# A decoder layer with a convolution branch and an attention branch: the order of the work around its norm and its output stage is changed

## The chip, the cores and the metric

The kernel runs on one core of one Trainium2 chip. The metric is the device time of one execution in microseconds (us). Times given as a median come from several executions without the profiler; everything that is read from a profile comes from one further execution, whose own time is given beside its span.

The core has a matrix engine (TensorE, PE in the profile), three elementwise engines (VectorE, DVE; ScalarE, ACT; GpSimd, POOL), a sequencer that issues most transfers (SyncE, SP), and DMA queues. Each engine works through its own list of instructions in order. An instruction that waits holds up all that stand behind it on its engine, and none on another engine unless they wait for its result.

## The reference, cut to what matters

Sequence length and model width are 1024, the batch is 1, all in float32.

```python
mod = c @ w_ada + b_ada
shift, scale, gate = split(mod, 3)
h = rmsnorm(x, norm_g) * (1 + scale) + shift
proj = h @ w_in
(glu_a, glu_b, z_conv, q, k, v, z_att, g_conv, g_att) = split(proj)

u = glu_a * sigmoid(glu_b)
u = causal_depthwise_conv(u, conv_w) + conv_b          # 31 taps for each channel
u = silu(layernorm(u, conv_ln_g, conv_ln_b))
y_conv = (u * silu(z_conv)) @ w_conv_out

q, k = rope(q, positions), rope(k, positions)
att = dilated_window_attention(q, k, v)                # 3 groups of 8 heads, width 64
y_att = (att * silu(z_att)) @ w_att_out

merged = sigmoid(g_conv) * y_conv + sigmoid(g_att) * y_att
out = rmsnorm(x + gate * (merged @ w_o), final_g)
```

## The kernel before, in words

**Products.** Every float32 operand of a projection is split into a high and a low part (`whi`/`wlo` of a weight, `hh`/`hl` of h, `uh`/`ul` of the conv branch), and a product is three matmuls: high by high, high by low, low by high (`mm3`, L72 to L75, and L605). A matmul is 128x128 by 128x512. Twelve of them, four blocks of the inner dimension by three products, make a **group**.

**Stages.** First h is built and the first projection units are computed together with it (to about 95 us). Then comes the middle stage (L420 to L1063, to about 610 us): all that is left of the conv branch, the gates and the values, the depthwise conv, the layernorm over channels and the product with `w_conv_out`. Attention and the last product follow; the change does not touch them.

**The middle stage** is a schedule written as code. `groups` is the list of PE groups in order, one for each step. `todo[step]` holds other work for a step, entered with `at(step, rank, fn)`; ranks run from EARLY over COPY, EVICT, HIGH, POOLED, POST_ to LOAD. `behind` holds generators (above all the conv of a channel tile on DVE, 31 taps each), which after each step are run on for a credit of one group; each piece yields its estimated price (`TAP` 1.33, `POST` 0.76), and `spend` takes from the same credit. So work put before a generator moves all its later pieces. The loop at the end runs step by step and writes every instruction into its engine's list in that order. The list is then fixed: an engine does not pass over an instruction that waits.

**Weights.** `Raw` loads a 128x1024 weight on SP into one of three `wraw` buffers. `Form` makes the split of one half of it: `whi` on ACT three steps before its use (L455), `wlo` on POOL two steps before (L458). Two `Form`s share one pair of tiles, and three pairs go round; a pair is free again when PE has read both halves.

**Around the start of the middle stage.** `first` holds six PSUM banks of the units computed so far, and `p_row` a seventh bank with the row of the shift. `first_units` (from L996) copies that row out on ACT (`gs`, L998), takes the sigmoids of four banks on ACT (L1002, L1005) and multiplies on DVE (`glu_half`, L670), which frees the banks. `t_first` loads combinations of h (`t_loads`, L500 to L504), adds them on DVE (`t_raws`, L508 to L511) and splits them: `t_high` on ACT (L515), `t_low` on DVE (L519). The first PE groups here (`plain`) need a bank that these free.

**The norm over channels.** `norm_mean` sums the eight conv results over channels on PE (`pm`, L775), `norm_squares` subtracts the mean on DVE, squares on ACT and adds up (`tot`, L785 to L793), `col_sums` brings the sums into columns (L128), `rstd_cols` makes 1/sqrt with a square root on ACT (L112) and six small operations on DVE (`lcols`, L113 to L117, L134), and eight transposes on PE spread them into `lrow` (L808). Then `norm_apply` makes for each of eight channel tiles: times `lrow` on DVE (L824), silu in two halves on ACT (L826), times the gate `sz` in two halves on DVE (L834), the high part `uh` on ACT (L837), the low part `ul` on POOL (L841).

**The output stage.** `first_outputs` runs eight steps of 12 matmuls; step k takes channel tile k into four banks (two output tiles d by two halves), so that PE can begin before all eight tiles are there. It needs four banks that the last `values` turn has just filled and that ACT must copy out (`gs`, L614). The six outputs left follow, four groups each. `Gated` multiplies a result by its gate `sgc` on DVE and stores it to `cscr`; it also loads a row block of `w_ada` into a `wraw` buffer and has DVE make the column of `gate` from it (`modulation`, L169) with `cb`, the conditioning vector in all partitions, which stands in slot t7. `tables` computes the sines for the rotation from `posi`.

## Time and profile before

| What | Value |
| --- | --- |
| Time of three runs, us | 1223.71, 1225.28, 1226.23 (median 1225.28) |
| The profiled execution: its time, its span, us | 1226.17, 1224.4 |
| Mean granted TensorE clock of it | 0.993 |
| PE busy, us and share of the span | 1197.1, 98% |
| DVE, ACT, POOL busy, us | 901.6, 587.2, 425.1 |

The profiled execution took 1.8 us more than its span, for what lies before its first and behind its last instruction. It stands 0.89 us above the median. In a row of the timeline the first number is the start in us from the beginning of the span, the second the duration in us, then come engine, line and operation; in brackets stands for how long the engine had been idle before, and which engine and tile ended that. A row with "x2" is two instructions, and its time covers both.

### The profile page before, as it was taken

How to read it: one execution, taken by the hardware profiler on the slowest of the kernel's cores; microseconds unless marked ns; L12 is line 12 of the kernel's file. 1: busy time of each engine (PE TensorE's matmuls, PEld its weight loads, DVE VectorE, ACT ScalarE, POOL GpSimd, SP SyncE). 2: the span in 40 equal slices, each digit the busy share in tenths (PEclk: the TensorE clock that was granted, in tenths of full speed). 3: DMA queues.
4: the chain of work that ended last, by engine and by line, in shares of the span. 5: the costliest groups of instructions: out<-in, count | busy, mean ns of one | idle time of the engine just before them, and what ended most of it. 6: DMA issues, size and time to landing. Idle time of an engine off the chain costs nothing.

```text
span 1224.4 us, 17342 instructions
## 1 busy us (share of the span) xinstructions
PE 1197.1 (98%) x6042; PEld 1000.4 (82%) x6042; DVE 901.6 (74%) x1488; ACT 587.2 (48%) x1209; POOL 425.1 (35%) x316
## 2 busy tenths in 40 slices
PE   9999999999999999898999999999999999999997
PEld 7886888888888887676888888888888888888886
DVE  7879999999999998565236657877877752549544
ACT  5655244544445345721025656656666564445111
POOL 0005868788787775632141011111111111200000
PEclk9999999999999999998999999999999999999999
DMA  9584323322423238536645455665675574668231
GB/s 358 194 321 138 121 97 110 105 82 89 130 68 133 84 137 304 194 126 218 223 114 154 122 147 137 184 167 145 166 190 145 136 194 132 215 225 291 86 103 69
DMA packets 100141, 194.49 MB, mean 159 GB/s; under 512 B 29587, under 2 KB 43219, under 8 KB 100054
## 3 DMA queue, kind: packets, MB, share of 16 engines
q1 hardware_dynamic: 83376, 186.77, 49.3%
q10 hardware_dynamic: 16678, 6.61, 1.9%
q8 instruction: 48, 0.79, 0.3%
q14 instruction: 39, 0.32, 0.1%
HBM read 122.25 MB, written 39.62 MB: 132 GB/s over the span
## 4 chain that ended last, share of the span: by engine, by line
PE 85%; DVE 6%; DMA 3%; ACT 2%; issue 2%; POOL 1%; SPq 0%; ACTq 0%; DVEq 0%; POOLq 0%
PE d L75 20%; PE d L73 20%; PE d L74 20%; PE d L605 4%; PE o L1345 4%; PE d L274 3%; PE s L1308 3%; PE t L1324 3%; PE d L1637 2%; PE d L1636 2%; PE d L1638 2%; DMA wraw<-in_w_co 1%; DVE tot L790 1%; ACT d L826 1%; DVE vt L824 0%
## 5 line engine op out<-in xcount | busy, mean ns | idle before, releaser
L547 DVE SCALAR_TENSOR_TENSOR acc<-u,cw,acc 128x1024 f32<-128x1024 f32 x232 | 298.8, 1288 | 6.6
L73 PE MATMUL d<-hh,whi 128*128 128x512 f32 x752 | 295.1, 392 | 2.4 <-ACT gs L998 1.3
L75 PE MATMUL d<-hh,wlo 128*128 128x512 f32 x752 | 293.6, 390 | 0.2 <-POOL wlo L58 0.2
L74 PE MATMUL d<-hl,whi 128*128 128x512 f32 x752 | 293.4, 390 | 0.0
L458 POOL TENSOR_TENSOR wlo<-wraw,whi 128x512 fp32r<-128x512 f32 x130 | 173.8, 1345 | 235.4 <-ACT whi L455 235.2
L58 POOL TENSOR_TENSOR wlo<-wraw,whi 128x512 fp32r<-128x512 f32 (+1 forms) x56 | 81.7, 1478 | 378.9 <-ACT whi L57 378.9
L75 PEld LDWEIGHTS d<-hh,wlo 128*128 128x128 f32 x752 | 141.1, 188 | 31.1 <-POOL wlo L58 0.6
L73 PEld LDWEIGHTS d<-hh,whi 128*128 128x128 f32 x752 | 141.4, 188 | 29.6 <-ACT gs L998 1.8
L74 PEld LDWEIGHTS d<-hl,whi 128*128 128x128 f32 x752 | 141.3, 188 | 26.0
L455 ACT ACTIVATE whi<-wraw 128x512 fp32r<-128x512 f32 x130 | 79.2, 624 | 120.0 <-DMA wraw<-in_w_co 58.4
L1317 ACT ACTIVATE sb<-sb,stats 128x128 f32<-128x128 f32 (+1 forms) x192 | 84.8, 443 | 31.5 <-DVE stats L1313 31.2
L1313 DVE CUSTOM_DVE_ANT_0 sb<-s,mask 128x128 f32<-128x128 f32 (+1 forms) x192 | 59.7, 349 | 52.6 <-PE s L1308 50.9
L1324 PE MATMUL t<-ident,sb 128*128 128x128 f32 x280 | 73.7, 276 | 0.0
L1345 PE MATMUL o<-ph,vt 128*64 128x128 f32 (+1 forms) x432 | 65.9, 253 | 0.0
L1139 ACT ACTIVATE ph<-t 128x384 fp32r<-128x384 f32 (+2 forms) x96 | 45.7, 476 | 38.9 <-PE t L1324 27.7
L1142 DVE TENSOR_TENSOR pl<-t,ph 128x384 fp32r<-128x384 f32 (+2 forms) x96 | 52.0, 542 | 11.0 <-ACT ph L1139 10.4
L73 PE MATMUL d<-uh,whi 128*128 128x512 f32 x128 | 52.0, 406 | 7.0 <-ACT whi L455 6.1
L1308 PE MATMUL s<-k,ql 128*128 128x128 f32 (+1 forms) x192 | 55.0, 292 | 0.0
L605 PE MATMUL d<-wlo,hh 128*128 128x512 f32 x128 | 50.7, 396 | 3.9 <-POOL wlo L458 3.9
L75 PE MATMUL d<-uh,wlo 128*128 128x512 f32 x128 | 51.8, 404 | 1.3 <-POOL wlo L458 1.1
L1345 PE MATMUL o<-pl,vt 128*64 128x128 f32 (+1 forms) x216 | 52.8, 261 | 0.0
L74 PE MATMUL d<-ul,whi 128*128 128x512 f32 x128 | 51.6, 403 | 0.0
(295 smaller groups left out, 2616.5 us busy)
## 6 DMA issues: line engine op xcount, KB each, us to landing
wraw<-in_w_t SPq DMA_DIRECT2D x67, 512.0 KB, 4.2
k<-kqp SPq DMA_DIRECT2D x96, 128.0 KB, 2.3
q<-kqp SPq DMA_DIRECT2D x96, 128.0 KB, 2.4
wraw<-in_w_v SPq DMA_DIRECT2D x19, 512.0 KB, 4.0
wa<-in_w_ada SPq DMA_DIRECT2D x16, 512.0 KB, 5.9
ql<-kqp SPq DMA_DIRECT2D x48, 128.0 KB, 2.4
wg<-wscr SPq DMA_DIRECT2D x48, 128.0 KB, 3.0
hscr<-x SPq DMA_DIRECT2D x8, 512.0 KB, 4.5
```

The source lines that it names most:

```text
L58: (lo_eng or nc.vector).tensor_sub(lo, raw, hi.bitcast(F32))
L73: nc.tensor.matmul(ps, lh, rh, start=start, stop=False, skip_group_check=again)
L74: nc.tensor.matmul(ps, lh, rl, start=False, stop=False, skip_group_check=again)
L75: nc.tensor.matmul(ps, ll, rh, start=False, stop=stop, skip_group_check=again)
L455: nc.scalar.activation(self.hi, src(), AF.Copy)
L458: nc.gpsimd.tensor_sub(self.lo, src(), self.hi.bitcast(F32))
L547: nc.vector.scalar_tensor_tensor(acc, u[:, k:k + S], cw[:, ct, k:k + 1], acc, op0=mult, op1=add)
L605: nc.tensor.matmul(ps[i], l[:, k, c], r, start=k == 0 and n == 0, stop=k == KT - 1 and n == 2)
L1308: products.append((w, lambda c=c, w=w, l=x[:, ts_], r=k[:, ks], i=i: nc.tensor.matmul(ps[:, c:c + w], l, r, start=i == 0, stop=i == 1)))
L1317: nc.scalar.activation(sb[:, c:c + w], sb[:, c:c + w], AF.Exp, bias=stats[:, t, h, 1:2], scale=-1.0, accum_out=stats[:, t, h, 0:1])
L1324: yield from ((lambda c=c: nc.tensor.transpose(ps[:, c:c + P], sb[:, c:c + P], ident)) for c in range(0, o, P))
L1345: nc.tensor.matmul(out_, l, r, **kw))
```

## The change

1. **Start of the middle stage.** `first_units` enters the four sigmoids first on ACT, then the `t_high` splits, then the copy of `p_row`. `t_low` is taken out of `t_first` and entered one step later, each with `spend(TAP)`. A one-element sigmoid is put in front of `t_loads`. `plain` takes its two banks in the other order. Slots of the pool are created in another order, and `t_loads` uses other slots.
2. **Norm.** A one-element square root is entered after the last square, and a one-element silu after the square root of the columns, each of which makes ACT load that function's table there.
3. **norm_apply.** The product with `lrow` of tile ct+1 is entered before the gate products of tile ct, its silu before the copy `uh` of tile ct; the `ul` subtractions are entered one step later.
4. **Weight forms.** The four halves of the first two `w_conv_out` tiles are paired by inner half (kh), no longer by output tile, and made at step + kh.
5. **Output stage.** The gate's column sums move out of `Gated` into `gate_sum`, which loads its part of `w_ada` into slot t7 and stands at step + 7 + 3d. The `sgc` loads are entered two steps later. `cb`, `posi`, `n_` and `m_` change their slots, and `cb` is loaded 12 steps earlier.

The core of the diff:

```diff
-    for x in ("n2", "n4", "h3", "l3"):
-        slot(x, "t")
-    piece("t", "gs", 4)
-    for x in ("n3", "s1", "sd0", "sd1", *(f"t{n}" for n in range(16))):
+    slot("h3", "t"), slot("l3", "t"), piece("t", "gs", 4)
+    for x in ("n3", "s1", "sd0", "sd1", "n2", "n4", *(f"t{n}" for n in range(16))):
         slot(x, "t")
...
-                if i == 0:
-                    ps[half] = bank()
+                if i == half == 0:
+                    ps[1], ps[0] = bank(), bank()
...
+        nc.scalar.activation(one_b[:, 0:1], ones[:, 0:1], AF.Sqrt)
         nc.vector.tensor_add(tot2, tot2, last)
...
         lcols = rstd_cols(pc, "l")
+        nc.scalar.activation(one_b[:, 0:1], ones[:, 0:1], AF.Silu)
...
         for ct in range(KT):
+            if ct + 1 < KT:
+                scaled_mul(ct + 1)
+                yield TAP
             for half in range(2):
                 s = wide(half)
                 nc.vector.tensor_mul(vt[ct][:, s], sg[half], sz_t[ct][:, s])
             yield 2 * POST
+            if ct + 1 < KT:
+                silu(ct + 1)
...
             nc.scalar.activation(hi, vt[ct], AF.Copy)
-            if ct + 1 < KT:
-                scaled_(ct + 1)
-                yield TAP
-            nc.gpsimd.tensor_sub(lo, vt[ct], hi.bitcast(F32))
             ch[ct], cl[ct] = hi, lo
+            at(now[0] + 1, POOLED, lambda ct=ct: nc.gpsimd.tensor_sub(cl[ct], vt[ct], ch[ct].bitcast(F32)))
...
-            at(step - 2, LOAD, self.load)
+            at(step, LOAD, self.load)
...
-            self.wa = load_raw(a["w_ada"][2 * KT + self.d])
...
+    def gate_sum(step, d):
+        box = []
+
+        def load():
+            box.append(slot("t7", "wada"))
+            nc.sync.dma_start(box[0], a["w_ada"][2 * KT + d])
+
+        def post():
+            modulation(2 * KT + d, gate_c[:, d:d + 1], box[0], box[0], cb_of[0])
+            spend(TAP)
+        at(step - 2, LOAD, load)
+        at(step, POST_, post)
...
-        raws = [Raw(step - 7 + d, a["w_co"][d]) for d in range(2)]
-        forms = {(d, kh): Form(step - 3 + 2 * kh + d, raws[d].half(kh)) for kh in range(2) for d in range(2)}
-        out = [Gated(step + 6 + d, d) for d in range(2)]
+        raws = [Raw(step - 7 + 2 * d, a["w_co"][d]) for d in range(2)]
+        forms = {(d, kh): Form(step + kh, raws[d].half(kh)) for kh in range(2) for d in range(2)}
+        out = [Gated(step + 5, d) for d in range(2)]
+        for d in range(KT):
+            gate_sum(step + 7 + 3 * d, d)
...
     def t_first():
+        nc.scalar.activation(one_b[:, 0:1], ones[:, 0:1], AF.Sigmoid)
         t_loads(0)
         t_raws(0)
-        for i in (1, 3, 2, 4):
-            t_high(i, 0)
-            t_low(i, 0)
...
     def first_units():
-        b_row = piece("gs", "gs", 4)[0:2]
-        nc.scalar.activation(b_row, p_row, AF.Copy)
-        nc.scalar.dma_start(bscr, b_row)
         sb = slot("n4", "sigb")
...
+        for i in (1, 3, 2, 4):
+            t_high(i, 0)
+        b_row = piece("gs", "gs", 4)[0:2]
+        nc.scalar.activation(b_row, p_row, AF.Copy)
+        nc.scalar.dma_start(bscr, b_row)
...
-    at(len(groups), LOAD, cb_load)
+    at(len(groups) - 12, LOAD, cb_load)
...
-    at(-1, HIGH, t_first)
+    at(-4, EARLY, t_first)
+    at(1, POST_, t_lows)
```

The lists of three engines show it. First ACT at the start of the middle stage, before: `t1h` to `t4h` are the splits, `gs` is the copy of `p_row`, `sigb` are the sigmoids.

```order
L455 ACTIVATE whi<-wraw 128x512 x2
L515 ACTIVATE t1h_855<-traw 128x1024
L515 ACTIVATE t3h_859<-traw 128x1024
L515 ACTIVATE t2h_863<-traw 128x1024
L515 ACTIVATE t4h_867<-traw 128x1024
L998 ACTIVATE gs<-d 2x512
L999 DMA bscr<-gs 2x512
L1002 ACT_TABLE_LOAD
L1002 ACTIVATE sigb<-d 128x512 x2
L1005 ACTIVATE sigb<-d 128x512 x2
```

The same place on ACT after the change.

```order
L453 ACTIVATE whi<-wraw 128x512 x2
L1016 ACT_TABLE_LOAD
L1016 ACTIVATE sigb<-d 128x512 x2
L1019 ACTIVATE sigb<-d 128x512 x2
L513 ACTIVATE t1h_862<-traw 128x1024
L513 ACTIVATE t3h_864<-traw 128x1024
L513 ACTIVATE t2h_866<-traw 128x1024
L513 ACTIVATE t4h_868<-traw 128x1024
L1023 ACTIVATE gs<-d 2x512
L1024 DMA bscr<-gs 2x512
```

The sigmoids and their table load moved ahead of the four splits, and the copy of `p_row` now stands behind both. The table load is still there.

Second, ACT from the square root of the columns (`ltmp`) to the fourth silu, before: `d<-vt` is a silu of two halves, `uh` a high part, `gs` are the copies that free the four banks of the last `values` turn.

```order
L112 ACTIVATE ltmp<-lcols 128x8
L455 ACTIVATE whi<-wraw 128x512 x2
L826 ACT_TABLE_LOAD
L826 ACTIVATE d<-vt_3697,cvec 128x512 x2
L837 ACTIVATE uh_3993<-vt_3697 128x1024
L826 ACTIVATE d<-vt_3699,cvec 128x512 x2
L455 ACTIVATE whi<-wraw 128x512 x2
L837 ACTIVATE uh_4022<-vt_3699 128x1024
L826 ACTIVATE d<-vt_3701,cvec 128x512 x2
L455 ACTIVATE whi<-wraw 128x512
L837 ACTIVATE uh_4048<-vt_3701 128x1024
L826 ACTIVATE d<-vt_3703,cvec 128x512 x2
```

And after the change.

```order
L112 ACTIVATE ltmp<-lcols 128x8
L803 ACT_TABLE_LOAD
L803 ACTIVATE one_b<-ones 128x1
L453 ACTIVATE whi<-wraw 128x512 x2
L832 ACTIVATE d<-vt_3694,cvec 128x512 x2
L832 ACTIVATE d<-vt_3696,cvec 128x512 x2
L848 ACTIVATE uh_4027<-vt_3694 128x1024
L453 ACTIVATE whi<-wraw 128x512 x2
L832 ACTIVATE d<-vt_3698,cvec 128x512 x2
L848 ACTIVATE uh_4056<-vt_3696 128x1024
L612 ACTIVATE gs<-d 128x512 x4
L832 ACTIVATE d<-vt_3700,cvec 128x512 x2
```

The table load moved ahead of the two weight splits, the silu of the next tile ahead of `uh`, and the four `gs` copies, which stood behind the fifth silu (two tiles further on), now stand behind the second `uh`. On PE the transposes into `lrow` moved: between them and the first matmul that reads `uh` there were 60 matmuls, and now there are 36, because the conv before the norm has moved two groups back (the `t_low` splits spend its credit).

Third, SP in the output stage, before: `sz` are the gates of the channel tiles, `w_co` the weights of the outputs, `w_ada` those of the gate sums.

```order
L892 DMA cb<-in_c 128x1024
L856 DMA posi<-in_positions 128x1024
L62 DMA wraw<-in_w_co 128x1024
L903 DMA sgc<-gcscr 128x1024
L62 DMA wraw<-in_w_ada 128x1024
L903 DMA sgc<-gcscr 128x1024
L62 DMA wraw<-in_w_ada 128x1024
L903 DMA sgc<-gcscr 128x1024
L62 DMA wraw<-in_w_ada 128x1024
L62 DMA wraw<-in_w_co 128x1024
L910 DMA cscr<-gs 128x512 x5
```

And after the change.

```order
L816 DMA sz<-szscr_103 128x1024
L62 DMA wraw<-in_w_co 128x1024
L864 DMA posi<-in_positions 128x1024
L911 DMA sgc<-gcscr 128x1024 x2
L924 DMA wada<-in_w_ada 128x1024
L62 DMA wraw<-in_w_co 128x1024
L917 DMA cscr<-gs 128x512 x4
L924 DMA wada<-in_w_ada 128x1024
L911 DMA sgc<-gcscr 128x1024
L917 DMA cscr<-gs 128x512
L62 DMA wraw<-in_w_co 128x1024
```

The third weight tile of `w_co` now follows the last `sz` directly, `cb` is gone from here, and between that tile and the fourth stands one `wada` load instead of three loads of `w_ada`, none of which uses a `wraw` buffer any more.

23 lines of the change are left out of this document (14 added, 9 removed).

## The prediction

> **What bounds the kernel now.** The profile's page says first that PE is busy for nearly the whole span, so the question is where PE loses time and how much of that the change can give back.
>
> ```profile
> PE 1197.1 (98%) x6042; PEld 1000.4 (82%) x6042; DVE 901.6 (74%) x1488; ACT 587.2 (48%) x1209; POOL 425.1 (35%) x316
> ```
>
> The view of PE's waits by line comes next (total us, times, longest us).
>
> ```profile
> PE d L73 <- ACT whi L455: 6.1, 2, 5.6
> PE d L605 <- POOL wlo L458: 3.9, 2, 3.4
> PE d L73 <- ACT gs L998: 1.3, 1, 1.3
> ...
> PE d L75 <- POOL wlo L458: 1.1, 1, 1.1
> PE d L73 <- DVE u L670: 1.1, 1, 1.1
> PE lrow L808 <- DVE lcols L117: 1.1, 1, 1.1
> PE d L73 <- ACT gs L614: 0.9, 1, 0.9
> ```
>
> Few waits, each met once or twice, and all of them at the places that the change touches. The table of windows (start:end, length, PE busy and its matmuls, granted clock, then DMA share and GB/s) puts them in time.
>
> ```profile
> 112.00:455.00 343.00, 343.00 (x1513) 1.00 0.31 103
> ...
> 500.00:530.00 30.00, 25.20 (x103) 0.94 0.32 106
> 530.00:560.00 30.00, 22.63 (x86) 0.90 0.60 211
> 560.00:605.00 45.00, 45.00 (x191) 0.95 0.61 194
> ```
>
> From 112 to 455 us PE never waits: 343 / 1513 = 0.227 us for a matmul, which is the steady price, and 12 of them, a group, take 2.72. From 500 to 605 the rows count 380 matmuls, some four of which lie across an edge and are counted twice. 376 x 0.227 = 85.4 of 105 us, so **19.6 us are lost there**. Only part of it is idle; the clock column says that the rest is slow matmuls after the waits.
>
> ```profile
> 558.01 0.80 PE L73 MATMUL d<-uh,whi 128*128 128x512 f32 x1 [5.61 <-ACT whi L455]
> ...
> 562.95 0.63 PE L74 MATMUL d<-ul,whi 128*128 128x512 f32 x1
> 563.37 0.63 PE L75 MATMUL d<-uh,wlo 128*128 128x512 f32 x1
> ```
>
> After a wait of 5.61 us matmuls still start 0.42 apart five us later. So the ceiling is 19.6 there, 1.1 for `lcols` at the norm before it, and at the start of the middle stage the two waits of 1.3 and 1.1 with some 0.2 of restart each: about 23.5 us in all. (`tot` is waited for as well, by less than the rows shown; its chain on DVE stays as it is, and I leave it in place.) No part of the change reaches the other stages.
>
> **Part 1, the start of the middle stage (90 to 112).** ACT and, around its wait, PE:
>
> ```profile
> 90.67 1.05 ACT L515 ACTIVATE t1h<-traw 128x1024 fp32r<-128x1024 f32 x1
> ...
> 95.91 1.06 ACT L515 ACTIVATE t4h<-traw 128x1024 fp32r<-128x1024 f32 x1 [1.18 <-DVE traw L511]
> 96.87 0.57 ACT L998 ACTIVATE gs<-d 2x512 f32<-2x512 f32 x1
> ...
> 97.77 1.28 ACT L1002 ACT_TABLE_LOAD   x1 [0.32 <-ACT gs L998]
> 99.06 1.09 ACT L1002 ACTIVATE sigb<-d 128x512 f32<-128x512 f32 x2
> 100.03 1.09 ACT L1005 ACTIVATE sigb<-d 128x512 f32<-128x512 f32 x2
> ```
> ```profile
> 97.50 0.50 PE L73 MATMUL d<-hh,whi 128*128 128x512 f32 x1 [1.30 <-ACT gs L998]
> ```
>
> PE's first wait is for the copy `gs` of `p_row`, its second for the product of unit and sigmoid. With the new order ACT has no idle time in this run: from 90.67 come table load 1.28, two pairs of sigmoids at 0.97 from start to start (1.94), four splits at 0.96 (95.91 to 96.87; 3.84), the copy 0.57, so the copy ends at 98.30 where it ended at 97.44. The splits wait for nothing, since DVE's last sum (L511, which ended t4h's wait at 95.91) is there before t4h's new turn. The first wait thus grows by 0.9. The second goes: the sigmoids are ready at 93.9, DVE's two products come right after its sum, at about 97.1, and PE wants that bank a group after 98.3. Its price was 1.1 and a restart of some 0.2. Saved: 1.3 - 0.9 = **0.4**, with ends of -0.9 (the second stays after all) and +2.8 (both go).
>
> The one-element sigmoid here is no preload. ACT takes a square root and other functions between it and the real sigmoids, and the list of after has a table load before those still. It adds one load of 1.28 near the start, beside DVE and PE work that has more than 2 us of room: nothing.
>
> The row 97.77 with the next start at 99.06 also gives a switch its price: 1.29. The Trainium skill, ScalarE: Activation LUTs, section "What ACT_TABLE_LOAD costs", adds a drain of about 1380 ns to the 1283 ns of the load; this trace does not show that drain. By the page the copy would come 1.4 us later still and this sum would end 1.4 us higher; by the row it does not.
>
> The `t_low` splits behind six conv taps are not wanted by PE before the values' groups, over 40 us on, and 112 to 455 shows how little PE depends on DVE's timing there: nothing.
>
> **Part 2, the norm (485 to 500).** `lrow` waited 1.1 on a chain in which ACT loaded the root's table (1.28 by the row above) behind the column sums. That load now comes earlier, so this wait goes: **1.2 saved** with its restart of 0.1. The silu's load likewise leaves the path to the first silu.
>
> **Part 3, from `lrow` to the first `uh` group.** This is the place that decides. `lrow` is done when PE goes on at L:
>
> ```profile
> 494.99 0.48 PE L605 MATMUL d<-whi,hh 128*128 128x512 f32 x1
> ```
> ```profile
> 500.02 1.49 ACT L826 ACTIVATE d<-vt,cvec 128x512 f32<-128x512 f32 x2
> 502.26 1.06 ACT L837 ACTIVATE uh<-vt 128x1024 fp32r<-128x1024 f32 x1 [0.76 <-DVE vt L834]
> 503.39 1.48 ACT L826 ACTIVATE d<-vt,cvec 128x512 f32<-128x512 f32 x2
> 504.82 1.13 ACT L455 ACTIVATE whi<-wraw 128x512 fp32r<-128x512 f32 x2
> ```
> ```profile
> 500.83 1.40 DVE L834 TENSOR_TENSOR vt<-d,sz 128x512 f32<-128x512 f32 x2 [4.34 <-ACT d L826]
> 502.14 1.21 DVE L824 TENSOR_TENSOR vt<-vt,lrow 128x1024 f32<-128x1024 f32 x1
> ```
> ```profile
> 503.40 2.36 POOL L841 TENSOR_TENSOR ul<-vt,uh 128x1024 fp32r<-128x1024 f32 x1 [10.57 <-ACT uh L837]
> 505.72 2.51 POOL L458 TENSOR_TENSOR wlo<-wraw,whi 128x512 fp32r<-128x512 f32 x2
> ```
>
> Before, the first silu came 5 us after L, and a tile took 3.37 (500.02 to 503.39). After, with these durations and nothing else in front: product with `lrow` to L+1.3, silu 0 to 2.9, gate products 0 to 3.65, silu 1 to 4.8, `uh0` to 5.8, two weight splits to 6.9, silu 2 to 8.4, `uh1` to 9.4, and only then the first `gs` copy, 0.5, to 10.0. On PE 36 matmuls take 8.2. The group of `uh0` needs `uh0` (5.8), `ul0` (5.85 + 2.36 = 8.2) and the banks that `gs` frees. So it starts at 10.0 in place of 8.2: **a new wait of 1.8, for `gs` and not for `uh` or `ul`**. The next: POOL's `wlo` pair to 10.75, `ul1` to 13.1, wanted at 13.0; silu 3 to 13.0 (the copies stand before it), `uh2` to 14.0, `ul2` to 16.4, wanted at 16.0: 0.1 and 0.4. From there a tile costs ACT 1.49 + 1.06 = 2.55, DVE 1.40 + 1.21 = 2.61, POOL 2.4, each below PE's 2.72, so nothing more. Together 2.3, and 0.6 for slow matmuls and restarts: between the 97.50 row (1.30 idle, then normal starts) and the 558 row. **The new loss is 2.9.**
>
> The Trainium skill, TensorE: Matmul & The Clock Gate, section "Part 1: The HAM clock gate", says that PE's clock halves after an idle window of about 3.4 us. By that a wait of 1.8 costs no slow matmul and the sum ends 0.6 lower; the 5.61 row agrees with the rule, and no row here has a lone wait near 1.8.
>
> **Part 4, weights and the output stage (500 to 605).** The old waits were for `wlo` (3.4), then `whi` 5.6 and 0.5, `wlo` 1.1, all for weights that came late: a tile pair mixed early and late halves, or the load stood late on SP:
>
> ```profile
> 550.36 0.33 SPq L62 DMA_DIRECT2D wraw<-in_w_co  x1
> ```
> ```profile
> 557.33 0.63 ACT L455 ACTIVATE whi<-wraw 128x512 fp32r<-128x512 f32 x1 [18.69 <-DMA wraw<-in_w_co]
> ```
>
> The fourth `w_co` was issued at 550.36 and split at 557.33, 7 us for a load beside other transfers, while PE stood. After, it stands behind the first `wada`, which waits for slot t7, freed when `ul7` is made: `ul2` at 16.4 and five tiles at 2.6 on, L+29.4. Issued soon after, landed 7 us later, split on ACT and POOL by L+39; PE wants it 96 + 48 matmuls (32.7 us) behind the start of `uh0`, with the waits above at about L+44. Five us of room. The third tile is issued behind the last `sz`, over 15 us before its use, and its first `wlo` on POOL ends 1.3 (half of the 2.51 row) after `ul7`, at L+30.7, PE wanting it at about L+33. Each later tile has a turn of 10.9 us on PE for its load. So all of it goes, and the 19.6 of these windows become 2.9: **16.7 saved**, with ends of 10 (one output wait of the old size, 5.61 and its slow matmuls, comes back) and 19.6.
>
> **Sum.** 0.4 + 1.2 + 16.7 = 18.3. 1226.17 - 18.3 = 1207.9 in place of the profiled execution; that stands 0.89 above the median of the runs, so I forecast **1207.0**.
>
> **Rivals.** (a) The cover of 36 matmuls fails by more: if DVE, ACT and POOL get in each other's way and a tile costs 3.37 as now, `ul` falls behind PE by 0.65 in each of seven tiles, 4.6 us, and slow clock with it, 2: 1207.0 + 6.6 = **1213.6**. For it: in the old loop every engine waits for another. Against: these waits (0.76, 0.85) come from an order that is undone. It decides once a tile costs over 2.72. (b) SP's head of line: `wada` behind `ul7`, or a store of results before a weight load, makes the fourth output tile late once more; the 5.61 wait with its slow matmuls, some 9 us, comes back: **1216**. It decides if that load lands over 12 us after `ul7`. (c) On the slow side: the conv now runs two groups later against everything that DVE also does, so the products that free PE's banks (L670 and the gates) stand one tap further back. A tap is this group:
>
> ```profile
> L547 DVE SCALAR_TENSOR_TENSOR acc<-u,cw,acc 128x1024 f32<-128x1024 f32 x232 | 298.8, 1288 | 6.6
> ```
>
> If each of the 16 pairs of units then waits one tap, 1.29, and 0.2 of restart, it costs 23.8: **1231**. For it: DVE spends 299 us on taps and stands idle only 6.6 before them. Against: in 343 us PE did not wait for it once. It decides where DVE's lead over PE is under one tap; with 12 of the 16 waits (18.3 / 1.49) the change gains nothing. (d) The change does not do what it says: the table loads land where they were and ACT's chain stays long. `lrow`'s 1.2 stays, and the load in front of the first silu puts 1.3 on the wait for `gs` and as much on the slow matmuls behind it: 3.8, **1211**. The lists speak against it, but for the sigmoid.
>
> **How the numbers follow.** Forecast 0.60, (a) 0.14, (b) 0.11, (c) 0.05, (d) 0.05; 0.05 for a gain that other waits eat up whole. The range runs from 1202.5 (the new 2.9 gone, and the start better by 1.6 of the 2.4 that it could be) to 1216 (rivals a, d and b's middle). It leaves out (c), the eaten gain and the upper half of (b), 0.16 in all. Below 0.2% (2.5 us) a difference cannot be told from none here. Faster 0.91, same 0.04, slower 0.05.
>
> **What would show it right or wrong.** Right: in PE's waits one row for `gs` L612 of 1.5 to 2.5, one for L1023 of about 2.1, none for `whi` or `wlo` over 0.5, none for `lcols`; silu rows at ACT about 2.6 apart; a clock of 1.00 from 530 on. Wrong: a wait for `ul` in several tiles (a), for `whi` in the output stage (b), for DVE between 112 and 455 (c), or an idle PE where no row of before had any.

## The result and the profile after

The changed kernel takes 1208.24 us (median of four runs, 1207.51 to 1211.77) where the kernel before takes 1225.33 (four runs): 0.9868 of it, with an interval of 0.9846 to 0.9890. The forecast was 1207.0, with a range from 1202.5 to 1216. The profiled execution of it took 1208.01 us, its span is 1206.2 us, 18.2 less than before.

PE's waits of the changed kernel, by line (total us, times, longest us):

```profile
PE d L73 <- ACT gs L1023: 2.2, 1, 2.2
PE d L143 <- ACT rrow L144: 1.6, 1, 1.6
PE d L73 <- ACT gs L612: 1.2, 1, 1.2
...
PE d L143 <- DVE xcols L117: 0.7, 1, 0.7
PE d L128 <- DVE tot L792: 0.6, 1, 0.6
PE d L274 <- DVE hl L241: 0.6, 1, 0.6
PE d L74 <- POOL ul L850: 0.2, 1, 0.2
PE d L75 <- POOL wlo L456: 0.2, 1, 0.2
```

The long rows of before are gone: `whi` 6.1, `wlo` 3.9 and 1.1, `u` 1.1, `lcols` 1.1. Two of the waits that the prediction announced are there, for the copy of `p_row` (L1023; 2.21, forecast about 2.1) and for the copies that free the banks (L612; 1.22, forecast 1.8). Three rows of the first stage are new or longer: `rrow` (0.9 before), `xcols` and `hl`. They were not forecast, and an idle PE where no row of before had any was one of the prediction's signs of being wrong. What causes them stays open: e3_nospend below has neither `xcols` nor `hl`, and a5_start, which lacks the one-element sigmoid, has an `xcols` of 0.8. The table of windows (start:end, length, PE busy and its matmuls, granted clock, DMA share, GB/s) shows the rest:

```profile
485.00:500.00 15.00, 14.40 (x66) 0.91 0.76 257
500.00:530.00 30.00, 28.55 (x126) 0.99 0.57 194
530.00:560.00 30.00, 30.00 (x134) 1.00 0.56 185
560.00:605.00 45.00, 45.00 (x200) 1.00 0.85 235
```

From 500 to 605 the rows count 460 matmuls where they counted 380, and the output stage runs at full clock without a pause. The window from 485 to 500 has a clock of 0.91, which was 1.00 at this place before. The wait for `tot` there is as long as before, but slow matmuls follow it:

```profile
494.20 1.95 PE L128 MATMUL d<-ones,tot 128*128 128x1 f32 x16 [0.60 <-DVE tot L792]
...
497.66 0.63 PE L603 MATMUL d<-whi,hh 128*128 128x512 f32 x1
```

Some seven matmuls here start 0.43 apart in place of 0.227, which costs 1.4 us. The last section shows that such slow matmuls behind a short wait depend on the execution.

**A measure for parts.** Attention took up to 6 us more in some profiled executions than in others, with the same lists (in e1_nosig below PE stood 3.6 us there for a DVE step, and DVE had waited 7 us for a gather), so times of single runs can't tell parts of 1 or 2 us apart. All kernels here have the same PE work, though, so I read from the one trace of each when PE reaches five places. Slow matmuls behind a short wait can move such a time by 1.4 to 1.6 us, and are named where they do. Times are in us from the start of the span; "uh0" is the first matmul that reads `uh`, "last" the last matmul of the output stage. Between `pm` and `lrow` lie the same matmuls in all; between `lrow` and `uh0` lie 60 in those with an asterisk and 36 in the others. "Lost" time below is the time from one matmul's start to the next, less 0.227. Each ratio is taken against executions of the kernel before in the same session (medians 1225.33 to 1226.58).

| Kernel | median, ratio to before (interval) | p_row's last matmul | pm | lrow | uh0 | last |
| --- | --- | --- | --- | --- | --- | --- |
| before* | 1225.3 | 95.81 | 466.74 | 494.17 | 515.58 | 615.60 |
| changed | 1208.24, 0.9868 (0.9846 to 0.9890) | 96.40 | 472.63 | 500.22 | 510.91 | 598.59 |
| e1_nosig | 1207.75, 0.9852 (0.9831 to 0.9873) | 95.96 | 472.11 | 499.99 | 510.46 | 598.16 |
| e2_row | 1207.43, 0.9832 (0.9814 to 0.9851) | 96.43 | 471.09 | 496.98 | 507.45 | 595.09 |
| e3_nospend* | 1212.78, 0.9891 (0.9870 to 0.9911) | 96.42 | 468.30 | 496.34 | 513.10 | 602.89 |
| a2_gate | 1212.01, 0.9884 (0.9863 to 0.9905) | 96.31 | 472.56 | 500.04 | 510.63 | 601.45 |
| a3_pipe | 1212.26, 0.9875 (0.9840 to 0.9911) | 96.39 | 474.21 | 500.80 | 511.95 | 601.48 |
| a4_tabs | 1209.16, 0.9852 (0.9822 to 0.9882) | 96.26 | 474.00 | 501.63 | 512.31 | 599.96 |
| a5_start* | 1210.19, 0.9863 (0.9831 to 0.9894) | 96.25 | 466.44 | 494.57 | 511.31 | 601.01 |
| b_forms* | 1223.57, 0.9972 (0.9956 to 0.9987) | 95.89 | 466.36 | 494.18 | 513.44 | 613.09 |
| b_gate* | 1214.89, 0.9904 (0.9878 to 0.9929) | 95.67 | 466.09 | 494.43 | 515.86 | 605.07 |
| b_pipe* | 1225.42, 0.9992 (0.9975 to 1.0009) | 95.97 | 466.63 | 495.54 | 516.19 | 615.59 |
| b_fg* | 1214.27, 0.9897 (0.9868 to 0.9927) | 96.05 | 466.55 | 493.02 | 512.31 | 602.32 |
| e5_best | 1206.14, 0.9833 (0.9810 to 0.9856) | 96.12 | 470.79 | 496.81 | 507.29 | 594.98 |

Of the 18.2 us, 17.0 lie before the last output matmul (615.60 to 598.59), and 1.2 in attention. By stretches, with 5.44 us of matmuls (24) allowed for that moved across `pm` and `lrow`: to `p_row` +0.59, to `pm` -0.14, to `lrow` +0.16, to `uh0` -5.28, through the output stage -12.34.

### The profile page after: what moved, and what is told of

It reads as the page before. It is cut to its first block, busy times and chain, and to the rows that moved or that the text cites. A ratio compares the mean times of both kernels' runs of the same rounds, so it can differ in the third digit from the quotient of the medians.

```text
span 1206.2 us, 17336 instructions
## 1 busy us (share of the span) xinstructions
PE 1189.1 (99%) x6042; PEld 996.1 (83%) x6042; DVE 905.1 (75%) x1488; ACT 586.7 (49%) x1213; POOL 429.2 (36%) x316
## 4 chain that ended last, share of the span: by engine, by line
PE 90%; DVE 3%; ACT 2%; DMA 2%; issue 1%; POOL 1%; SPq 0%; DVEq 0%; ACTq 0%; POOLq 0%
PE d L73 23%; PE d L74 23%; PE d L75 23%; PE o L1370 4%; PE d L603 4%; PE s L1333 3%; PE t L1349 3%; PE d L1661 2%; PE d L1662 2%; PE d L1663 2%; DMA wraw<-in_w_v 1%; PE d L274 1%; ACT hh L238 1%; DVE hl L241 1%; DVE tot L788 1%
## 5 line engine op out<-in xcount | busy, mean ns | idle before, releaser
L73 PEld LDWEIGHTS d<-hh,whi 128*128 128x128 f32 x752 | 141.4, 188 | 29.1 <-ACT gs L1023 2.7
L1164 ACT ACTIVATE kqp<-rot 128x512 fp32r<-128x512 f32 x24 | 23.1, 964 | 64.4 <-DVE rot L1187 39.0
L1661 PE MATMUL d<-oh,hh 128*128 128x512 f32 (+1 forms) x136 | 51.2, 377 | 0.0
L1663 PE MATMUL d<-oh,hl 128*128 128x512 f32 (+1 forms) x136 | 51.2, 377 | 0.0
```

The lines of the kernel that those rows point to most:

```text
L73: nc.tensor.matmul(ps, lh, rh, start=start, stop=False, skip_group_check=again)
L1661: nc.tensor.matmul(ps, hh[:, k, c], rh, start=k == 0, stop=False)
```

## Experiments on the start of the middle stage

**e1_nosig.** The changed kernel without its one-element sigmoid.

```diff
     def t_first():
-        nc.scalar.activation(one_b[:, 0:1], ones[:, 0:1], AF.Sigmoid)
         t_loads(0)
```

> The changed kernel without the one-element sigmoid in front of t_loads; nothing else differs. Theory A (read from the two traces): the sigmoid's table load, 1.28 us at 11.7 us of the span, sits in front of the high split of the second tile of h, which starts 0.58 later, and every later step of that stage keeps that lag (square root of the columns at 46.58 for 46.02). Without it the time falls by 0.57, to about 1207.7 where the changed kernel has 1208.24, and PE reaches the first group of the middle stage at about 96.0 in place of 96.6. Theory B (as the prediction had it): the load lies in slack and costs nothing: 1208.2 within 0.2, PE arrives as in the changed kernel.

ACT's timeline of the changed kernel near the start of the span:

```profile
11.71 1.28 ACT L1005 ACT_TABLE_LOAD   x1
13.01 0.20 ACT L1005 ACTIVATE one_b<-ones 128x1 f32<-128x1 f32 x1
13.12 1.14 ACT L238 ACTIVATE hh<-x,gcol 128x1024 fp32r<-128x1024 f32 x1
```

And that of the kernel before:

```profile
12.54 1.15 ACT L238 ACTIVATE hh<-x,gcol 128x1024 fp32r<-128x1024 f32 x1 [0.85 <-DVE gcol L233]
```

The load fills an idle time of 0.85 and reaches 0.58 beyond it. Without it p_row's last matmul stands 0.44 earlier (95.96 for 96.40), and the last output matmul 0.43. This is theory A, with 0.44 where it said 0.57 (the whole of that trace had started 0.2 late, as its first `hh` shows). All the traces bear it out: counted from the first `hh` split of each, p_row's last matmul comes 87.20 to 87.48 us later in the six that have the sigmoid and 86.77 to 86.99 in the eight that lack it. "Nothing" was wrong: this preload costs about half a us, and the table is loaded again before the real sigmoids.

**e2_row.** The changed kernel with the copy of `p_row` ahead of the splits.

```diff
-        for i in (1, 3, 2, 4):
-            t_high(i, 0)
         b_row = piece("gs", "gs", 4)[0:2]
         nc.scalar.activation(b_row, p_row, AF.Copy)
         nc.scalar.dma_start(bscr, b_row)
+        for i in (1, 3, 2, 4):
+            t_high(i, 0)
```

> The changed kernel with the copy of p_row put ahead of the four t_high splits, behind the sigmoids. Theory A: PE's wait of 2.21 is for that copy alone, which has the four splits (3.84) in front of it; with the copy at about 95.0 PE, which arrives at 96.6, does not wait for it, DVE's product for the next bank is there by 98, so 2.4 us go: about 1205.8. Theory B: another wait takes its place, since the splits themselves, now 0.5 later, or DVE's product are next: the gain is under 1.0, 1207.2 or more, and PE's list of waits shows u L668 or t_h in its place.

ACT in the changed kernel, where the copy stands behind everything:

```profile
97.43 1.07 ACT L513 ACTIVATE t4h<-traw 128x1024 fp32r<-128x1024 f32 x1
98.38 0.57 ACT L1023 ACTIVATE gs<-d 2x512 f32<-2x512 f32 x1
```

PE's waits in e2_row:

```profile
PE d L73 <- ACT gs L1021: 0.7, 1, 0.7
```

The wait fell from 2.2 to 0.7, and nothing took its place; the rest stays because the copy can't begin before p_row's last matmul has ended. Neither theory had that bound: 1.5 of the 2.4 us went. The last output matmul came 3.5 earlier. Of the other 2, 1.4 are the slow matmuls behind `tot` in the changed kernel, which did not occur in this execution, and 0.3 a wait for `tot` of 0.3 for 0.6; the edit's own part is thus about 2.

**a5_start.** The changed kernel with the start of the middle stage put back as before (ACT's order, the `t_low` splits, no one-element sigmoid; the slots and the order of the two banks stay changed). A part of the edit:

```diff
     def first_units():
+        b_row = piece("gs", "gs", 4)[0:2]
+        nc.scalar.activation(b_row, p_row, AF.Copy)
+        nc.scalar.dma_start(bscr, b_row)
         sb = slot("n4", "sigb")
...
-    at(-4, EARLY, t_first)
-    at(1, POST_, t_lows)
+    at(-1, HIGH, t_first)
```

> The changed kernel with the start of the middle stage as before (copy of p_row first, sigmoids last, t_low with t_high, no one-element sigmoid); norm, loop, forms and gate slot stay changed. Theory A: the start itself was worth nothing (two waits of 1.3 and 1.1 for one of 2.21, less 0.57 of the sigmoid's load), and without the spent credit the norm stands two groups earlier, with gs behind the fourth uh: the gs wait grows by 1 to 2. In sum 1208.2 to 1210. Theory B: sooner sigmoids matter for the conv, which starts 4 us sooner with the change: 1210 to 1212, with new waits of PE between 112 and 485.

The two old waits came back, shorter (`gs` 0.7, `u` 1.0), `pm` stands at 466.44 as in the kernel before, and PE waits for no more between 112 and 485 than it did there. At the norm the wait for `gs` L612 is 2.1 for 1.2, and the last output matmul stands 2.4 later. Of that, 1.6 are slow matmuls behind this wait (clock 0.50 from 511.24 to 514.65), which the same wait does not have in e3_nospend. This is theory A in kind; the time is 0.2 over the upper end of what it said. So the new start is worth nothing by itself; what it brings is a norm two groups later, and the next experiment shows by itself that this is a gain.

**e3_nospend.** The changed kernel without the credit that the `t_low` splits spend.

```diff
     def t_lows():
         for i in (1, 3, 2, 4):
             t_low(i, 0)
-            spend(TAP)
```

> The changed kernel without the spend(TAP) in t_lows, so that the norm stands two groups earlier on PE again: 60 matmuls between lrow and the first uh group, not 36. Theory A (the order on ACT decides): the four gs copies of the last values turn then stand behind the fourth uh on ACT, which is done at about L+15.5 to L+16 (L is the end of lrow), while PE wants the banks at L+13.6: a wait of 2 to 3 for gs L612 in place of 1.22, so the time rises by about 1 to 2 us, to 1209 to 1210.5. Theory B (the shorter cover is what costs): with 5.4 us more cover the waits for gs (1.22) and ul (0.23) go, 1.8 us less: about 1206.4.

ACT of e3_nospend around the copies that free the banks:

```profile
510.11 1.47 ACT L832 ACTIVATE d<-vt,cvec 128x512 f32<-128x512 f32 x2
511.52 1.04 ACT L848 ACTIVATE uh<-vt 128x1024 fp32r<-128x1024 f32 x1
512.47 2.02 ACT L612 ACTIVATE gs<-d 128x512 f32<-128x512 f32 x4
```

And its waits of PE at the norm and in the output stage:

```profile
PE d L73 <- ACT gs L612: 2.1, 1, 2.1
...
PE d L75 <- POOL wlo L456: 1.1, 2, 0.6
...
PE d L73 <- ACT whi L453: 0.8, 1, 0.8
```

Theory B falls: 24 matmuls more of cover made it slower, by 4.3 us at the last output matmul. The copies have a fixed step, the loop over channel tiles does not; when the loop begins two groups sooner, ACT has more of its work in front of the copies, and PE gets its banks later against its own list (2.25 lost for 1.38, from the starts around the wait). Waits for weights in the output stage, 1.9, come with it. Another 1.6 is not the edit's: behind the same wait of 2.21 at 99 us matmuls were slow in this execution and not in the changed kernel's. That leaves 2.7 for the edit, more than the 1 to 2 of theory A, which had no waits for weights.

## Experiments on the norm and the output stage

**a4_tabs.** The changed kernel without the one-element square root and silu.

```diff
-        nc.scalar.activation(one_b[:, 0:1], ones[:, 0:1], AF.Sqrt)
         nc.vector.tensor_add(tot2, tot2, last)
...
         lcols = rstd_cols(pc, "l")
-        nc.scalar.activation(one_b[:, 0:1], ones[:, 0:1], AF.Silu)
```

> The changed kernel without the one-element square root and silu, so that ACT loads each table at its first real use. Theory A: lrow waits again about 1.1 behind the root's load, and the silu's load (1.28) stands in front of the first silu and puts about 0.3 to 1.3 on the wait for gs: 1.5 to 2.6 us slower, 1209.7 to 1210.8. Theory B: ACT has idle time in front of both (1.90 and 3.63 in the changed kernel's trace), so the loads fit in there: within 0.5, 1208.2 to 1208.7.

ACT of a4_tabs:

```profile
493.23 1.13 ACT L453 ACTIVATE whi<-wraw 128x512 fp32r<-128x512 f32 x2
494.38 1.28 ACT L112 ACT_TABLE_LOAD   x1
497.78 0.21 ACT L112 ACTIVATE ltmp<-lcols 128x8 f32<-128x8 f32 x1 [2.12 <-DVE lcols L134]
```

This is theory B. The load is an instruction of its own; here it runs as soon as ACT reaches it, 3.4 us before its square root, and the silu's load at 499.06 runs 5.1 us before its silu. That is not so in every kernel. In b_forms below the silu's load stands behind ACT's wait for DVE's product, although ACT idles ahead of it:

```profile
496.55 1.28 ACT L826 ACT_TABLE_LOAD   x1 [5.58 <-DVE vt L824]
497.84 1.49 ACT L826 ACTIVATE d<-vt,cvec 128x512 f32<-128x512 f32 x2
```

It does in b_fg too (4.11 of idle time). There a preload could take the load's 1.28 off the way to the first silu; no run tries it. In a4_tabs PE has no wait for `lcols`, and from `pm` to `lrow` it takes 27.63 us for 27.59 with the preloads, from there to `uh0` 10.68 for 10.69. The last output matmul stands 1.37 later, and all of that is there at `pm` already: slow matmuls behind the wait at 99 us. So the two preloads bring nothing in the changed kernel.

**b_forms.** The kernel before with the new weight forms alone.

```diff
-        raws = [Raw(step - 7 + d, a["w_co"][d]) for d in range(2)]
-        forms = {(d, kh): Form(step - 3 + 2 * kh + d, raws[d].half(kh)) for kh in range(2) for d in range(2)}
+        raws = [Raw(step - 7 + 2 * d, a["w_co"][d]) for d in range(2)]
+        forms = {(d, kh): Form(step + kh, raws[d].half(kh)) for kh in range(2) for d in range(2)}
```

> The kernel before with one part of the change alone: the four weight halves of the first two outputs made at step + kh in pairs of their own, and their loads at step - 7 + 2d. Theory A: the waits for wlo at 507 (3.39, with slow matmuls behind 5.0) and at 512 (0.49) came from the pairs in which a half of the last values weights and a half of an output weight lay together; they go, and the waits in the output stage (whi 5.6, wlo 1.1) stay: about 5 us faster than before, 1220. Theory B: the norm's loop is late by as much, PE waits for ul or gs instead, and the time stays within 1.5 of 1225.3.

PE's waits in b_forms:

```profile
PE d L73 <- ACT whi L455: 7.4, 1, 7.4
PE d L73 <- ACT gs L614: 2.0, 1, 2.0
PE d L605 <- POOL wlo L458: 2.0, 2, 1.3
```

The result lies between the theories: 2.5 us less at the last output matmul. The `lcols` wait went here, with no table preloaded. The waits for `wlo` fell from 3.9 to 2.0, so the pairing of the halves is not their whole cause. But `gs` grew from 0.9 to 2.0, and the late weight load waits longer for having been met sooner: 7.4.

**b_gate.** The kernel before with the gate sums in their own slot, and the slots and steps that belong to it.

```diff
-        cb_of.append(slot("t7", "cb"))
+        cb_of.append(slot("s1", "cb"))
...
-            self.wa = load_raw(a["w_ada"][2 * KT + self.d])
...
-        out = [Gated(step + 6 + d, d) for d in range(2)]
+        out = [Gated(step + 5, d) for d in range(2)]
+        for d in range(KT):
+            gate_sum(step + 7 + 3 * d, d)
...
-    at(len(groups), LOAD, cb_load)
+    at(len(groups) - 12, LOAD, cb_load)
```

> The kernel before with the output stage's part of the change alone: gate sums in slot t7 (with cb, posi and the two work tiles in their new slots, cb 12 steps sooner, sgc two steps later); norm, loop, weight forms and start stay as before. The last output matmul stands at 615.6 us in the kernel before and at 598.6 in the changed one. Theory A: the shared wraw buffers and cb at the head of SP's list made the third and fourth w_co tile late; both waits (0.65 and 1.30 at 538 to 540; 5.77 at 558) go with their slow matmuls, some 13 us less at the last output matmul, the waits at 507 to 516 stay: marker 603 to 605, time about 1213. Theory B: putting this part back into the changed kernel cost only 2.9, so the part is worth about 3 and the rest of the wait is the tile pair that PE frees late: marker 611 to 613, about 1222.

This is theory A, at the edge of what it said: the last output matmul at 605.07, 10.5 earlier. All of it lies in the output stage, whose waits are down to 0.42, 0.79 and 0.64 of lost time, while `wlo` at 507 stays (3.4). ACT of b_gate also shows where the wait for `lcols` comes from (1.7 here):

```profile
491.09 0.63 ACT L455 ACTIVATE whi<-wraw 128x512 fp32r<-128x512 f32 x1 [4.48 <-DMA wraw<-in_w_co]
491.74 1.28 ACT L112 ACT_TABLE_LOAD   x1
493.03 0.21 ACT L112 ACTIVATE ltmp<-lcols 128x8 f32<-128x8 f32 x1
```

The square root's table load stands behind the split of a `w_co` half that had to wait for its transfer. The new forms put the split of a `w_v` half there, for which ACT has no wait (in b_forms the load stands at 486.72, directly behind the split); with them the wait for `lcols` is gone in every kernel.

**b_fg.** Both of these parts in the kernel before; of the edits, the two lines that matter most:

```diff
+        forms = {(d, kh): Form(step + kh, raws[d].half(kh)) for kh in range(2) for d in range(2)}
...
+            gate_sum(step + 7 + 3 * d, d)
```

> The kernel before with weight forms and gate slot together, nothing else. Theory A: forms alone gave 2.5 at the last output matmul (with a longer whi wait, 7.5, in place of the shorter ones) because the output stage took part of it back; with the gate slot that wait goes too, so the two give 12 to 15: marker 601 to 603.5, within 3 of the kernel with all but the loop changed (601.5). Theory B: loop and table loads carry a good part of the gain: marker over 605.

This is theory A: the last output matmul stands at 602.32, 13.3 earlier, where the two alone gave 2.5 and 10.5. `lrow` to `uh0` takes 19.29 as with the forms alone, the output stage 90.01 for 100.02. PE's waits there:

```profile
PE d L605 <- POOL wlo L458: 2.0, 2, 1.3
PE d L73 <- ACT gs L614: 2.0, 1, 2.0
```

**b_pipe.** The kernel before with the new loop order alone.

```diff
         for ct in range(KT):
+            if ct + 1 < KT:
+                scaled_mul(ct + 1)
+                yield TAP
...
+            if ct + 1 < KT:
+                silu(ct + 1)
...
-            if ct + 1 < KT:
-                scaled_(ct + 1)
-                yield TAP
-            nc.gpsimd.tensor_sub(lo, vt[ct], hi.bitcast(F32))
+            at(now[0] + 1, POOLED, lambda ct=ct: nc.gpsimd.tensor_sub(cl[ct], vt[ct], ch[ct].bitcast(F32)))
```

> The kernel before with the new order in norm_apply's loop alone (product with lrow and silu of the next tile ahead, ul entered a step later). Theory A: with 60 matmuls of cover the loop was not what PE waited for; wlo at 507 (3.56) and the output stage's waits come from the weights and stay, at most 1.5 us go: marker 614 to 615.6, time 1224 to 1225. Theory B: the loop's 3.4 us for a tile made everything behind it late, POOL's splits too, so 4 us or more go: marker under 611.6.

This is theory A by the time: the last output matmul stands at 615.59 and has not moved. By the waits it is neither theory. Theory A said that `wlo` stays at 3.56, but it fell to 1.4, and the gain came back as waits for `gs` (2.6), `lcols` (2.3) and `whi` (7.5).

**a3_pipe.** The changed kernel with the old loop, the same edit the other way:

```diff
-                scaled_mul(ct + 1)
...
-                silu(ct + 1)
...
+                scaled_(ct + 1)
...
+            nc.gpsimd.tensor_sub(lo, vt[ct], hi.bitcast(F32))
```

> The changed kernel with norm_apply's loop in the old order (silu of the next tile behind uh, ul entered in the same step); forms, gate slot and table loads stay changed. Theory A: a tile costs 3.37 again, over PE's 2.72, so PE waits for ul about 0.65 in each of six or seven tiles: 4 to 4.6 us of waits, and some 2 of slow matmuls, and the first wait (gs, ul0) grows too: about 1214 to 1216. Theory B: the weights, not the loop, were what PE waited for: with them in time the old loop costs under 1.5: 1208.2 to 1209.7.

PE's waits in a3_pipe:

```profile
PE d L73 <- ACT gs L612: 1.9, 1, 1.9
...
PE d L128 <- DVE tot L792: 1.0, 1, 1.0
...
PE d L74 <- POOL ul L847: 0.6, 1, 0.6
```

From `lrow` to the last output matmul it takes 100.68 for 98.37: 2.3 us. There is one wait for `ul` of 0.6, not one in each tile. That is neither theory's size. Of the 2.3, 1.6 are slow matmuls behind the wait for `gs` (clock 0.50 from 513.22 to 516.63), which the wait of 1.2 in the changed kernel does not have. The rest of its 2.9 is slow matmuls at 99 us less what the norm gained.

**a2_gate.** The changed kernel with `w_ada` back in the `wraw` buffers, and with it the `sgc` loads and the gate sums at their old steps. A part of the edit:

```diff
-            at(step, LOAD, self.load)
+            at(step - 2, LOAD, self.load)
...
             nc.sync.dma_start(self.sg, gcscr[self.d])
+            self.wa = load_raw(a["w_ada"][2 * KT + self.d])
```

> The changed kernel with the gate sums put back into Gated: w_ada is loaded into the wraw buffers again, two steps before the outputs, and summed on DVE behind each output; all else stays changed. Theory A: the wraw buffers that hold w_ada wait for DVE's gate sums, so the fourth w_co tile is issued about 19 us late as before and PE waits 5 to 6 for whi with slow matmuls behind: 8 to 10 us slower than the changed kernel, about 1217. Theory B: that wait came from the late norm, not from the shared buffers; with the norm 10 us earlier on SP's list it is gone anyway: 1208.2 to 1210.

It costs 2.9 us at the last output matmul, all in the output stage. That lies between the theories, nearer to B. SP of a2_gate:

```profile
515.01 0.42 SPq L864 DMA_DIRECT2D posi<-in_positions  x1
...
537.61 0.33 SPq L62 DMA_DIRECT2D wraw<-in_w_co  x1
```

Its DVE and ACT:

```profile
535.16 1.28 DVE L916 TENSOR_TENSOR gs<-d,sgc 128x512 f32<-128x512 f32 x2
536.36 1.21 DVE L169 CUSTOM_DVE_ANT_0 wraw<-wraw,cb 128x1024 f32<-128x1024 f32 x1
```
```profile
544.94 1.15 ACT L453 ACTIVATE whi<-wraw 128x512 fp32r<-128x512 f32 x2 [19.12 <-DMA wraw<-in_w_co]
```

The fourth weight tile still waits for a buffer that DVE's sum gives back, but that sum ends 12.8 us sooner than before. The DVE rows of the kernel before show why it was late there:

```profile
535.92 0.69 DVE L859 CAST n__4203<-posi 128x1024 f32<-128x1024 int32 x1 [9.14 <-DMA posi<-in_positions]
...
547.91 1.28 DVE L908 TENSOR_TENSOR gs<-d,sgc 128x512 f32<-128x512 f32 x2
549.11 1.22 DVE L169 CUSTOM_DVE_ANT_0 wraw<-wraw,cb 128x1024 f32<-128x1024 f32 x1
```

`cb` in slot t7 had to wait for `ul7` (POOL, to 530.4), `posi` stood behind it on SP, DVE stood 9 us for `posi` and did 12 us of table work before it came to the gate products and the sum that freed the buffer. With `cb` loaded ahead into a slot that is free, `posi` is issued at 515 and the chain is undone, shared buffers or not. That splits the gate part, worth 10.5 alone, into about 3 for the buffers and the rest for the head of SP's list; this split leans on two kernels that differ in the norm as well, and no run moves `cb` alone, so it is read from the rows and not shown.

**e5_best.** The changed kernel with the edits of e1_nosig and e2_row together:

```diff
-        nc.scalar.activation(one_b[:, 0:1], ones[:, 0:1], AF.Sigmoid)
...
         nc.scalar.activation(b_row, p_row, AF.Copy)
         nc.scalar.dma_start(bscr, b_row)
+        for i in (1, 3, 2, 4):
+            t_high(i, 0)
```

> The changed kernel without the one-element sigmoid and with the copy of p_row ahead of the t_high splits. Theory A: both gains add, 0.4 to 0.6 of the start and 1.5 of the wait for the copy (which can't begin before p_row's last matmul): the last output matmul at 594.5 to 596.7 in place of 598.6, the time at 1205 to 1206.5. Theory B: the two share one cause (ACT's list before the copy), so the sum is not over 1.6: marker 597 or later.

The last output matmul stands at 594.98, 3.6 before the changed kernel's; the time is 1206.14 us, 0.9833 of before with an interval of 0.9810 to 0.9856. Of the 3.6, 0.3 come before p_row's last matmul and 1.5 from the shorter wait for the copy. Another 1.4 is luck of this execution: the slow matmuls behind `tot` are absent, as in e2_row (see the last section). Without it the last output matmul would stand at 596.4, still within theory A and earlier than theory B allows. By the times alone its interval and the changed kernel's overlap; by the traces the edits remove what they were meant to.

The forms part was not taken out of the changed kernel by itself: by my reading of the lists, with the new place of `ul` in POOL's list the old forms would make POOL and PE wait for each other. No run shows this.

## Why the prediction was right, and where its steps were not

**The start.** The forecast was 0.4 saved, by a first wait that grows and a second that goes. The trace has one wait of 2.21, as forecast, and 2.49 of lost time for 2.93 before: 0.44 saved. The step on the one-element sigmoid failed. It named "DVE and PE work that has more than 2 us of room" as its cover; ACT itself was on the path there, with 0.85 us of idle time for 1.48 us of work, and the price was about 0.5. The room was looked for on the engines that wait, and not at the next instruction of the same list. The drain of about 1380 ns that the Trainium skill puts behind each table load (ScalarE: Activation LUTs, section "What ACT_TABLE_LOAD costs") is not in the traces after the change either: 13.01 follows 11.71 + 1.28.

**The norm.** The forecast was 1.2 saved because the root's table is loaded ahead. The wait went, but for another reason, and b_gate, b_forms and a4_tabs show it: ACT came late to the root's table load because a weight split ahead of it waited for a transfer. The new forms took that away. In the changed kernel the preloads are worth 0.0; whether they alone would have ended the wait in the kernel before, no run shows. The saving was then eaten by slow matmuls behind the `tot` wait (1.4), so this stretch is 0.16 longer in the profiled execution. No step of the prediction had that, and the last section shows that it hangs on the execution: e2_row and e5_best do not have them.

**From `lrow` to `uh0`.** The forecast was a new wait of 1.8 for `gs` and 0.5 for `ul`, 2.9 with slow matmuls. The trace has 1.22 and 0.23, and 2.4 lost around them with restarts. No slow matmuls followed the wait for `gs` here; behind waits of 1.9 (a3_pipe) and 2.1 (a5_start) at the same place they did. The chain held: counted from PE's going on at 501.24, the `gs` copies begin at L+9.0 (forecast 9.4), the first `uh` group starts at L+9.7 (10.0). POOL's last `ul` ends at 530.3, L+29.1 (29.4):

```profile
510.28 2.02 ACT L612 ACTIVATE gs<-d 128x512 f32<-128x512 f32 x4
```
```profile
510.91 0.50 PE L73 MATMUL d<-uh,whi 128*128 128x512 f32 x1 [1.22 <-ACT gs L612]
```
```profile
514.79 15.52 POOL L850 TENSOR_TENSOR ul<-vt,uh 128x1024 fp32r<-128x1024 f32 x6 [0.46 <-ACT uh L848]
```

A tile costs ACT 2.36 and not 2.55, since neighbours on ACT overlap: a pair of silus and the copy behind it start 1.41 and 0.95 after one another's start, with 1.48 and 1.06 of duration. So the copies come 0.4 sooner than forecast, and that is a part of the over-estimate in the term of 2.9. What the step did not see is that the place of the copies on ACT and the shorter cover belong together: e3_nospend, with the longer cover, is slower.

**The output stage.** The forecast was that all of its waits go. They did: no wait over 0.2 from 530 to 605. The fourth weight tile was issued at 530.72 and split at 535.28, 4.6 us for the load (forecast: up to 7), over 8 before its use. The cause that was named, a load that stands late on SP, is shown by a2_gate and b_gate; that the larger part of the lateness went over `posi` and DVE's table work, as the rows under a2_gate have it, was not seen.

**The sum.** The forecast was 18.3 off the profiled execution, and the measured difference is 18.16 (1226.17 to 1208.01). The output stage and the way to it gave 17.6 (forecast 16.7). The way to p_row's last matmul lost 0.6 against an expected nothing, the stretch from there to `pm` gained 0.1 against 0.4, the norm lost 0.2 against an expected gain of 1.2, and 1.2 came from attention, which the prediction had left out. That the sum agrees to 0.2 is therefore partly luck: attention varies by up to 6 us between executions, and its 1.2 makes up for the losses. By the medians the gain is 17.1, 1.2 less than forecast.

**The rivals.** Rival (a) did not occur: silu rows stand 2.36 apart. Rival (b), the head of SP's list, was no risk with 8 us to spare. Rival (c): PE lost 0.36 once between 112 and 455, for `wlo`, and nothing for DVE. Rival (d) was right on the one-element sigmoid: the table is loaded again before the real sigmoids. The other two loads did move ahead in ACT's list, and a4_tabs shows that nothing hung on them here.

**Single parts do not add.** Taken out one by one, gate, loop and preloads cost 2.9, 2.3 and 0.0, with the start 2.4: 7.6 of 17, of which 3.2 (1.6 each for loop and start) are slow matmuls that depend on the execution. Put in one by one, gate, forms and loop give 10.5, 2.5 and 0.0. The forms' and the loop's gains were handed on to the same late weight load (`whi` 7.4 and 7.5 in place of 5.6), and only with the gate part does PE keep them.

## What to carry to other kernels

Where PE stands for one late transfer, every gain ahead of it turns into a longer wait at that place: look for the wait that ends last, and follow it back over queues and buffers, here from a weight over a shared buffer, DVE's order and a position table to a load that needed slot t7 before it was free. A table load needs no preload where ACT reaches it well ahead of its use, so look in the trace on which side of ACT's idle time it stands (a4_tabs and b_forms differ); a preload is work in ACT's list and has to be covered there. More distance between producer and consumer on one engine's list helps only if what stands between on the other engine's list keeps its place.

## What the runs showed of the hardware that was not expected

- The same wait of 2.21 us at 99 us was followed by matmuls at full speed in the changed kernel (clock 1.00 in the window from 92 to 112, 78 matmuls), e1_nosig and a2_gate, and by matmuls 0.43 apart in e3_nospend, a3_pipe and a4_tabs (clock 0.91, 71 or 72 matmuls), 1.6 us. So a wait of a given length has two prices here, and the granted clock shows what decides. From 92 us to the end of the middle stage the clock in these traces is 1.00 or 0.50; a stretch of 0.50 lasts 3.41 us or two or three times that, and the stretches of one execution begin whole multiples of 3.41 apart (506.50, 540.63 and 557.70 in the kernel before). This grid lies elsewhere in each execution. In the three traces with slow matmuls the whole wait lies in one step of it, with PE busy for 1.20 or 1.21 of 3.41 us, and the next step is slow. In the other three an edge of the grid cuts the wait (PE busy 2.31 and 2.31, 2.86 and 1.75, 2.60 and 2.01 in the two steps), and no step is slow. First e3_nospend, then the changed kernel, whose grid is counted back from its slow stretch at 497.25:

```profile
96.27:99.68 3.41, 1.20 (x6) 1.00 0.64 193
99.68:103.09 3.41, 3.41 (x10) 0.50 0.97 318
```
```profile
94.48:97.89 3.41, 2.31 (x11) 1.00 0.42 127
97.89:101.31 3.42, 2.31 (x10) 1.00 0.80 210
```

The wait for `tot` of 0.60, with 16 one-column matmuls behind it, goes the same way: in the changed kernel nearly all of it lies in the step from 493.84 to 497.25, and slow matmuls follow; in the kernel before, e2_row and e5_best an edge cuts it (at 489.43, 493.55 and 492.97), and none follow. The Trainium skill, TensorE: Matmul & The Clock Gate, section "Part 1: The HAM clock gate", tells of a window of 3.4 us that runs free of the kernel; the grid agrees with that. Its idle time of a whole window is more than these waits had, and the rows decide. How busy a step must be to keep the clock, these rows do not settle.

- DVE operations on 8 columns take 0.17 us, but 1.23 and 1.19 in a4_tabs where POOL split weights at the same time (498.59 to 501.10). The Trainium skill, SBUF — State Buffer, section "SBUF: two separate sides", says that DVE and GpSimd share a port pair which, for the operations that need it, the one that starts first holds for its whole instruction; these rows agree, each of the two taking about as long as one POOL split (1.25).

```profile
498.46 0.17 DVE L115 TENSOR_TENSOR ltmp<-ltmp,lcols 128x8 f32<-128x8 f32 x1
498.66 1.23 DVE L116 TENSOR_SCALAR ltmp<-ltmp 128x8 f32<-128x8 f32 x1
```
